# Strassen's two-term sums in the second MLP product of a hybrid decoder layer, with the down weights' sums formed as they are loaded

## The chip, the cores and the metric

The kernel runs on one core of a Trainium2 chip. The metric is the time of one execution on the device in microseconds (us). Three executions of the kernel before took 1248.96 to 1250.3 us, with a median of 1249.71. The engines named below are PE (TensorE, matrix products), DVE (VectorE), ACT (ScalarE), POOL (GpSimd) and SP (SyncE, which issues most DMA transfers).

## The reference

The reference is one layer of a decoder: a normalization, a projection into attention and state-space heads, both mixers, an output projection with a residual, and a squared-ReLU MLP with a second residual. Sequence length and model width are 1024, the hidden width of the MLP is 4096, all in float32. The change lies in the last line.

```python
def _hybrid_layer(x, ...):
    xn = _rmsnorm(x, norm1_g)
    proj = xn @ w_in
    ...
    x = x + mix @ w_out
    hdn = jnp.square(jax.nn.relu(_rmsnorm(x, norm2_g) @ w_mlp_up))
    return x + hdn @ w_mlp_down
```

## The kernel before

The kernel is written as a dataflow over tiles. A planner of the framework, which runs before the program is loaded, turns it into one fixed list of instructions per engine: it takes the instructions in the order of the program as priorities, simulates them with its own costs of operations and transfers, and puts each on its engine's list where the simulation has it ready. An instruction may thus stand far ahead of its place in the program, as early as its tile is free in the simulation. Waits between engines are semaphores that the framework adds. Its costs and due times are not in the trace; the order that came out is.

Every float32 operand of a product is split into a high and a low part (`split`, L77 to L79: ACT copies the high part at L78, DVE subtracts it from the value at L79), and every product of two operands is three matmuls, high by high, high by low, low by high (`mm3`, L106 to L108). All of this is the same before and after.

**Up product** (`up_proj`, run for 16 blocks of 256 hidden features). The product of the up weights with the normalized activations is done in Winograd's form of Strassen's scheme: 2 x 2 blocks, seven products in place of eight. A block loads its up weights as two raw tiles `wm` (L853; the pool `rawp` has two tiles), forms sums of them on DVE (L903, L909, L914, L919), and runs seven products of 12 matmuls each over 512 columns (`psz`, `psx`, `psy`). The activations' sums `X` lie in tiles 0 to 13 of the pools `big_a` and `big_b`. `staggered` interleaves the blocks: the first product of block b+1 stands before the last of block b.

The products give the four quarters of the hidden block, `c11`, `c12`, `c22`, `c21`, each 128 features by 512 tokens. `stage` and `hidden` (L871, L879 to L881) copy, add, and apply the squared ReLU; `keep` (L875) stores a tile to DRAM from POOL's queue. Seven tiles per block are stored, in `d_a[n][i]`: the four quarters or sums of them, as the down product needs them (`comb`, L885, and an addition in place, L923).

In the same function the **down weights** are made ready: a block's rows of `w_down` are loaded as one tile `wd` of 1 MB (L891, issued by SP, in tiles 14 and 15 by turns), four subtractions in place on DVE (L907, L912, L917, L925) turn its quarters into Winograd's sums, and the tile is stored to DRAM as `d_t` (L926, issued by POOL).

**Down product** (`down_proj`). Again seven products, each of 8 steps over pairs of blocks. A step loads two operands of 512 KB each (L973: stored hidden tiles, L974: a quarter of the raw weights or of `d_t`), both into one tile `raw` of 1 MB. Twelve such tiles turn (`RAW`: 14 and 15, then the tiles of `X` as block 15's products let go of them). ACT and DVE split both operands into tiles `ud` (128 x 1024 elements each; the pool `wp` has five tiles), and PE runs 24 matmuls into four PSUM banks. After the last step of a product `gather` (L999) adds each of the four banks to rows of the output tile `x2`, and where the output is done SP stores it (L1001). The residual `x2` is loaded in eight transfers (L1011) after the first step. The first step is placed before block 15's last product.

Of the kernel before, what the change touches and what calls it, by code (L numbers as in the profile page):

```python
# [8 lines left out]
F32 = mybir.dt.float32  # L9
F32R = mybir.dt.float32r  # L10
AF = mybir.ActivationFunctionType
OP = mybir.AluOpType
# [22 lines left out]
def hybrid_layer_kernel(ctx: ExitStack, tc: tile.TileContext, io: dict, out: bass.AP):  # L35
    nc = tc.nc
    PE, ACT, DVE, POOL = nc.tensor, nc.scalar, nc.vector, nc.gpsimd

    consts = ctx.enter_context(tc.tile_pool(name="consts", bufs=1))
    dram = ctx.enter_context(tc.tile_pool(name="dram", bufs=1, space=bass.MemoryType.DRAM))  # L40
    rawp = ctx.enter_context(tc.tile_pool(name="rawp", bufs=2))
    wp = ctx.enter_context(tc.tile_pool(name="wp", bufs=5))
# [4 lines left out]
    for nm, (o, shp) in PACK.items():  # L47
        n = math.prod(shp)
# [18 lines left out]
    d_x2 = [dram.tile([128, 1024], F32, name=f"d_x2{t}") for t in range(8)]  # L67

    d_a = [[dram.tile([2, 128, 512], F32, name=f"d_a{n}_{i}") for i in range(7)] for n in range(8)]
    d_t = [dram.tile([2, 128, 2, 1024], F32, name=f"d_t{n}") for n in range(8)]  # L70

    def rsqrt(out_, in_, mul, n):
        v = consts.tile([128, 8], F32, tag="rsq", name="rsq", bufs=4)
# [3 lines left out]
    def split(h, l, src, eng=DVE):  # L77
        ACT.activation(h, src, AF.Copy)  # L78
        eng.tensor_tensor(l, src, h.bitcast(F32), op=OP.subtract)  # L79
# [45 lines left out]
    def place(n, shape, dtype, name):  # L125
        return (big_a if n < 6 else big_b[0]).tile(shape, dtype, tag=f"g{n}", name=name)
# [720 lines left out]
    HS, H3 = 2, 4  # L847
    def up_proj(blk):

        raw = []  # L850
        for kh in range(2):
            r = rawp.tile([128, 1024], F32, tag="raw", name=f"wm{blk}_{kh}")
            nc.sync.dma_start(out=r, in_=io["w_up"][blk, :, kh])  # L853
# [13 lines left out]

        def stage(tag, ps=None):
            st = half(tag, "st")
            if ps is not None:  # L870
                ACT.activation(st, ps, AF.Copy)  # L871
            return st

        def keep(i, st):
            POOL.dma_start(out=d_a[blk // 2][i][blk % 2], in_=st)  # L875

        def hidden(st, ps):
            if ps is not None:
                DVE.tensor_tensor(st, st, ps, op=OP.add)  # L879
                ACT.activation(st, st, AF.Relu)  # L880
            ACT.activation(st, st, AF.Square)  # L881

        def comb(tag, i, a, b):
            o = half(tag, "comb")
            DVE.tensor_tensor(o, a, b, op=OP.subtract)  # L885
            keep(i, o)
            return o


        wd = place((14, 15)[blk % 2], [128, 2, 1024], F32, f"wd{blk}")  # L890
        nc.sync.dma_start(out=wd, in_=io["w_down"][blk])  # L891
        b11, b12, b21, b22 = wd[:, 0, :512], wd[:, 0, 512:], wd[:, 1, :512], wd[:, 1, 512:]

        z = tr_bank("psz")
        prod(z, a12, B21, True, HS if blk == 0 else 4)
        yield
        x = s_bank("psx")
        prod(x, a11, B11, True, HS if blk == 0 else 4)
        c11 = stage("t", x)
        hidden(c11, z)  # L900
        keep(0, c11)
        yield
        DVE.tensor_tensor(a21, a21, a22, op=OP.add)  # L903
        y = mm_bank("psy")
        prod(y, a21, T1, True, H3 if blk == 0 else 4)
        c22 = stage("x2", y)
        DVE.tensor_tensor(b12, b12, b11, op=OP.subtract)  # L907
        yield
        DVE.tensor_tensor(a21, a21, a11, op=OP.subtract)  # L909
        prod(x, a21, T2, False)  # L910
        c12 = stage("xs", x)
        DVE.tensor_tensor(b22, b22, b12, op=OP.subtract)  # L912
        yield
        DVE.tensor_tensor(a12, a12, a21, op=OP.subtract)  # L914
        prod(y, a12, B22, False)
        hidden(c12, y)
        DVE.tensor_tensor(b11, b22, b11, op=OP.subtract)  # L917
        yield
        DVE.tensor_tensor(a11, a22, a21, op=OP.subtract)  # L919
        prod(x, a11, T3, False)  # L920
        hidden(c22, x)
        keep(2, c22)
        DVE.tensor_tensor(c12, c12, c22, op=OP.add)  # L923
        keep(3, c12)
        DVE.tensor_tensor(b21, b21, b22, op=OP.subtract)  # L925
# [12 lines left out]
    def staggered(gens):  # L938
# [18 lines left out]
    def half_unit():  # L957
# [2 lines left out]
            halves.extend((u[:, 1], u[:, 0]))  # L960
        return halves.pop()

    x2 = []
    RAW = (14, 15, 2, 3, 0, 1, 8, 6, 7, 9, 4, 5)
    X2 = (10, 11, 12, 13)

    def down_proj():


        def prod(ps, i, b, start, after=None):  # L970
            for n in range(8):
                raw = place_turn(RAW, [128, 2, 2, 512], F32, "raw")
                nc.sync.dma_start(out=raw[:, 0], in_=d_a[n][i].rearrange("b p m -> p b m"))  # L973
                nc.sync.dma_start(out=raw[:, 1], in_=b(n))  # L974
                u = []
                for o in range(2):
                    u.append(wp.tile([128, 2, 2, 512], F32R, tag="w", name="ud"))
                    split(u[o][:, 0], u[o][:, 1], raw[:, o])
                ua, ub = u
                for pos in range(4):  # L980
                    pp = slice(pos * 128, pos * 128 + 128)
                    for f in range(2):
                        mm3(ps[pos], ua[:, 0, f, pp], ua[:, 1, f, pp], ub[:, 0, f], ub[:, 1, f],
                            start and n == 0 and f == 0, n == 7 and f == 1, not start)
                    if n == 7:
                        for g in after:
                            gather(ps, pos, *g)
                yield

        def wq(kh, dh):  # L990
            return lambda n: io["w_down"][2 * n:2 * n + 2, :, kh, dh * 512:dh * 512 + 512].rearrange("b p m -> p b m")

        def tq(kh, dh):
            return lambda n: d_t[n][:, :, kh, dh * 512:dh * 512 + 512].rearrange("b p m -> p b m")

        def gather(ps, pos, th, dh, last=False):
            t = 2 * pos + th
            cc = slice(dh * 512, dh * 512 + 512)
            DVE.tensor_tensor(x2[t][:, cc], x2[t][:, cc], ps[pos], op=OP.add)  # L999
# [12 lines left out]
        yield from p2  # L1012
# [77 lines left out]
```

## Time and profile before

| what | value |
|---|---|
| median of three executions | 1249.71 us |
| the profiled execution | 1249.52 us |
| its span, first to last instruction | 1247.7 us |
| mean granted clock of PE | 0.957 |
| busy share of the span: PE, DVE, ACT, POOL | 92%, 66%, 48%, 29% |
| DMA moved in the span | 239.73 MB, 192 GB/s |
| first up-weight split, last matmul of the up product | 586.6 us, 944.2 us |
| first and last matmul of the down product | 936.2 us, 1243.4 us |

The profile is that of one execution. Its page gives busy time per engine, a picture of the span in 40 slices, the DMA queues, the chain of work that ended last, and groups of instructions by line, engine and tile. Other views list single instructions in order of time, total waits of one engine for another, and sums over stretches of time. A busy PE is not PE at its peak: matmuls overlap, so the count of matmuls per microsecond says more than the busy share. A name such as `raw<-d_a` reads: tile `raw` written from `d_a`.

### The profile page before, as it was taken

To read this page: it belongs to the slowest core of one execution; us is meant where nothing else is said; L and a number is where in the kernel's file an instruction comes from. 1 tells how busy PE (TensorE), PEld (TensorE's weight loads), DVE (VectorE), ACT (ScalarE), POOL (GpSimd) and SP (SyncE) were. 2 spreads that over 40 slices of the span, in tenths; PEclk is the share of its full clock that TensorE was granted. 3 is DMA by queue.
4 is the path that set the end of the run, shared out by engine and by line. 5 is a ranking of instruction groups with operands and counts; after the bars stand their busy time and mean duration, and the time that the engine had idled before them with its cause. 6 is when DMAs were issued, how large, how long until landed. Compare 5 with 4: busy or idle time off the path is not lost.

```text
span 1247.7 us, 16686 instructions
## 1 busy us (share of the span) xinstructions
PE 1148.6 (92%) x5734; PEld 961.9 (77%) x5734; DVE 818.2 (66%) x1553; ACT 599.2 (48%) x1276; POOL 363.4 (29%) x544
## 2 busy tenths in 40 slices
PE   6766989999999999999798789999999999999998
PEld 4555777898998887778687567888888888888887
DVE  7998875667666687668887666656554554554453
ACT  5221243777777785434545444555553333333332
POOL 6595732444545464123321112112111000000000
PEclk9887886999999999899999989999999999999999
DMA  7733441635353426654589887444459966555500
GB/s 283 285 101 95 150 132 42 211 140 167 138 203 111 160 97 211 209 185 160 197 312 360 290 323 270 146 150 166 147 213 401 385 216 217 191 184 197 169 34 34
DMA packets 94821, 239.73 MB, mean 192 GB/s; under 512 B 8720, under 2 KB 27664, under 8 KB 85776
## 3 DMA queue, kind: packets, MB, share of 16 engines
q1 hardware_dynamic: 76560, 149.94, 35.7%
q0 software_dynamic: 16736, 85.99, 18.5%
q10 hardware_dynamic: 1440, 2.73, 0.6%
q8 instruction: 45, 0.74, 0.2%
q14 instruction: 40, 0.33, 0.1%
HBM read 164.74 MB, written 73.89 MB: 191 GB/s over the span
## 4 chain that ended last, share of the span: by engine, by line
PE 60%; DVE 12%; DMA 10%; issue 8%; POOL 5%; ACT 4%; SPq 0%; ACTq 0%; POOLq 0%; DVEq 0%
PE psx L107 7%; PE psx L108 7%; PE psx L106 7%; PE psy L106 4%; PE psy L107 4%; PE psy L108 4%; DMA wm<-in_w_up_dram 3%; PE pso L576 3%; PE psq L108 2%; PE psq L106 2%; PE psq L107 2%; PE pss L542 2%; PE psz L106 2%; DMA d_t<-wd 2%; PE psz L107 2%
## 5 line engine op out<-in xcount | busy, mean ns | idle before, releaser
L79 DVE TENSOR_TENSOR ud<-raw,ud 128x1024 fp32r<-128x1024 f32 x112 | 133.0, 1222 | 156.7 <-ACT ud L78 156.7
L78 ACT ACTIVATE ud<-raw 128x1024 fp32r<-128x1024 f32 x112 | 113.0, 1053 | 187.9 <-PE psx L108 103.6
L106 PE MATMUL psx<-X,wu 128*128 128x512 f32 (+1 forms) x260 | 101.9, 392 | 9.3 <-ACT st L871 6.8
L108 PE MATMUL psx<-X,wu 128*128 128x512 f32 (+1 forms) x260 | 101.5, 390 | 0.5 <-DVE wu L79 0.5
L107 PE MATMUL psx<-X,wu 128*128 128x512 f32 (+1 forms) x260 | 101.2, 389 | 0.7 <-DVE X L79 0.7
L78 ACT ACTIVATE wu<-wm 128x512 fp32r<-128x512 f32 x112 | 67.3, 626 | 70.6 <-DMA wm<-in_w_up_dram 37.1
L106 PE MATMUL psx<-ud 128*128 128x512 f32 x256 | 99.6, 389 | 0.0
L107 PE MATMUL psx<-ud 128*128 128x512 f32 x256 | 99.6, 389 | 0.0
L108 PE MATMUL psx<-ud 128*128 128x512 f32 x256 | 99.6, 389 | 0.0
L106 PE MATMUL psq<-wq,xt 128*128 128x384 f32 x256 | 93.4, 365 | 0.7 <-DMA xt<-d_x 0.6
L79 DVE TENSOR_TENSOR wu<-wm,wu 128x512 fp32r<-128x512 f32 x112 | 75.7, 695 | 25.9 <-ACT wu L78 25.9
L875 POOL DMA_DIRECT2D d_a<-st x64 | 34.6, 540 | 198.8 <-ACT st L881 185.6
L107 PE MATMUL psq<-wq,xt 128*128 128x384 f32 x256 | 90.6, 354 | 0.3 <-DVE wq L83 0.3
L108 PE MATMUL psq<-wq,xt 128*128 128x384 f32 x256 | 90.8, 354 | 0.0
L106 PEld LDWEIGHTS psx<-X,wu 128*128 128x128 f32 x260 | 49.3, 189 | 21.9 <-ACT st L871 8.1
L550 POOL TENSOR_SCALAR s<-s,dn 128x128 f32<-128x128 f32 (+3 forms) x64 | 50.2, 788 | 47.8 <-DVE dn L549 45.8
L106 PE MATMUL psy<-X,wu 128*128 128x512 f32 x128 | 52.2, 408 | 10.5 <-ACT st L871 10.5
L79 DVE TENSOR_TENSOR pt<-psp,pt 128x128 fp32r<-128x128 f32 (+2 forms) x96 | 51.1, 552 | 16.0 <-ACT pt L78 15.3
L576 PE MATMUL pso<-pt,V 128*128 128x256 f32 x320 | 54.8, 295 | 3.3 <-ACT pt L78 1.8
L107 PEld LDWEIGHTS psx<-X,wu 128*128 128x128 f32 x260 | 49.3, 190 | 10.9 <-DVE X L79 0.9
L108 PEld LDWEIGHTS psx<-X,wu 128*128 128x128 f32 x260 | 49.3, 190 | 10.7 <-DVE wu L79 0.7
L880 ACT ACTIVATE st<-st 128x512 f32<-128x512 f32 x48 | 30.2, 630 | 53.5 <-DVE st L879 52.7
(306 smaller groups left out, 3116.0 us busy)
## 6 DMA issues: line engine op xcount, KB each, us to landing
xt<-d_x POOLq DMA_DIRECT2D x30, 1024.0 KB, 5.2
raw<-d_a SPq DMA_DIRECT2D x56, 512.0 KB, 4.1
wm<-in_w_up_dram SPq DMA_DIRECT2D x32, 512.0 KB, 4.4
wd<-in_w_down_dram SPq DMA_DIRECT2D x16, 1024.0 KB, 6.5
d_t<-wd POOLq DMA_DIRECT2D x16, 1024.0 KB, 6.8
d_a<-st POOLq DMA_DIRECT2D x64, 256.0 KB, 3.6
raw<-d_t SPq DMA_DIRECT2D x32, 512.0 KB, 5.0
d_a<-comb POOLq DMA_DIRECT2D x48, 256.0 KB, 4.8
```

The source lines that it names most:

```text
L78: ACT.activation(h, src, AF.Copy)
L79: eng.tensor_tensor(l, src, h.bitcast(F32), op=OP.subtract)
L106: PE.matmul(ps, lhsT=ah, rhs=bh, start=start, stop=False, skip_group_check=more)
L107: PE.matmul(ps, lhsT=ah, rhs=bl, start=False, stop=False, skip_group_check=more)
L108: PE.matmul(ps, lhsT=al, rhs=bh, start=False, stop=stop, skip_group_check=more)
L542: PE.matmul(ps[:, :cw], lhsT=Qd[a][:, h, b * 128:(b + 1) * 128], rhs=K2[:, h, c0:c0 + cw], start=a == 0, stop=a == 1)
L550: POOL.tensor_scalar(s[:, :n], s[:, :n], dn, 1.0, op0=OP.mult, op1=OP.mult)
L576: PE.matmul(po[:, :256], lhsT=V2[:, k0 + kb, h, :], rhs=pt[:, a, kb, :], start=k0 + kb == 0 and a == 0, stop=k0 + kb == nb - 1 and a == 1)
L875: POOL.dma_start(out=d_a[blk // 2][i][blk % 2], in_=st)
L880: ACT.activation(st, st, AF.Relu)
```

## The change

The second product goes from Winograd's form to Strassen's own, in which no sum has more than two terms. With H for the hidden quarters (first index token half, second feature half) and B for the weights' quarters the seven products are now

- H11 (B12 - B22)
- H22 (B21 - B11)
- (H21 - H11) (B11 + B12)
- (H11 + H12) B22
- (H21 + H22) B11
- (H11 + H22) (B11 + B22)
- (H12 - H22) (B21 + B22)

In `up_proj` the load of `wd`, its four subtractions and the store to `d_t` are gone, and `d_t` with them. The hidden tiles stored are still seven per block; five of them are now sums (four were before). Two of the sums get tiles of their own (`o1`, `o2`), three are written in place over `c12`, `c11` and `c22`; `c11` and `c22` have been stored themselves before that.

In `down_proj` the tile `raw` is cut into two units of 512 KB (`raw_unit`). A step loads one unit of hidden values, one of weights and, in five of the seven products, a second one of weights, which DVE adds to or subtracts from the first (128 x 1024 elements) before the split. The order of the products is the one of the list. Three products gather to two quarters of the output and four to one, so that there are 40 gathers instead of 28. The first product accumulates in the banks that the third one goes on with; the last two share theirs.

```diff
-    d_t = [dram.tile([2, 128, 2, 1024], F32, name=f"d_t{n}") for n in range(8)]
...
-        def comb(tag, i, a, b):
-            o = half(tag, "comb")
-            DVE.tensor_tensor(o, a, b, op=OP.subtract)
+        def comb(i, o, a, b, op):
+            DVE.tensor_tensor(o, a, b, op=op)
             keep(i, o)
-            return o
-
-        wd = place((14, 15)[blk % 2], [128, 2, 1024], F32, f"wd{blk}")
-        nc.sync.dma_start(out=wd, in_=io["w_down"][blk])
-        b11, b12, b21, b22 = wd[:, 0, :512], wd[:, 0, 512:], wd[:, 1, :512], wd[:, 1, 512:]
...
-        DVE.tensor_tensor(b12, b12, b11, op=OP.subtract)
...
-        DVE.tensor_tensor(b22, b22, b12, op=OP.subtract)
...
         hidden(c12, y)
-        DVE.tensor_tensor(b11, b22, b11, op=OP.subtract)
+        comb(N21M11, half("xs", "o1"), c12, c11, SUB)
         yield
...
         hidden(c22, x)
-        keep(2, c22)
-        DVE.tensor_tensor(c12, c12, c22, op=OP.add)
-        keep(3, c12)
-        DVE.tensor_tensor(b21, b21, b22, op=OP.subtract)
-        POOL.dma_start(out=d_t[blk // 2][blk % 2], in_=wd)
-        s2 = comb("xs", 4, c12, c11)
-        comb("x2", 5, c22, s2)
+        keep(N22, c22)
+        comb(N21P22, c12, c12, c22, ADD)
+        comb(N11P22, half("x2", "o2"), c11, c22, ADD)
         yield
         prod(x, a22, T4, False)
         c21 = stage("t")
         ACT.activation(c21, x, AF.Relu)
         hidden(c21, None)
-        keep(1, c21)
-        comb("t", 6, c21, s2)
+        comb(N11P12, c11, c11, c21, ADD)
+        comb(N12M22, c22, c21, c22, SUB)
         yield
...
+        def raw_unit(src):
+            if not spare:
+                r = place_turn(RAW, [128, 2, 2, 512], F32, "raw")
+                spare.extend((r[:, 1], r[:, 0]))
+            r = spare.pop()
+            nc.sync.dma_start(out=r, in_=src)
+            return r
...
-        def prod(ps, i, b, start, after=None):
+        def prod(ps, i, b0, b1, op, start, to):
             for n in range(8):
-                raw = place_turn(RAW, [128, 2, 2, 512], F32, "raw")
-                nc.sync.dma_start(out=raw[:, 0], in_=d_a[n][i].rearrange("b p m -> p b m"))
-                nc.sync.dma_start(out=raw[:, 1], in_=b(n))
-                u = []
-                for o in range(2):
-                    u.append(wp.tile([128, 2, 2, 512], F32R, tag="w", name="ud"))
-                    split(u[o][:, 0], u[o][:, 1], raw[:, o])
-                ua, ub = u
+                ra = raw_unit(d_a[n][i].rearrange("b p m -> p b m"))
+                rb = raw_unit(wd(n, *b0))
+                if b1 is not None:
+                    DVE.tensor_tensor(rb, rb, raw_unit(wd(n, *b1)), op=op)
+                ua, ub = [wp.tile([128, 2, 2, 512], F32R, tag="w", name="ud") for _ in range(2)]
+                split(ua[:, 0], ua[:, 1], ra)
+                split(ub[:, 0], ub[:, 1], rb)
...
-        z = l_banks("psz")
-        p2 = prod(z, 1, wq(1, 0), True, [(0, 0)])
-        next(p2)
+        b11, b12, b21, b22 = (0, 0), (0, 1), (1, 0), (1, 1)
+        x = l_banks("psx")
+        m3 = prod(x, N11, b12, b22, SUB, True, [(0, 1, ADD)])
+        next(m3)
         yield
...
-        x = r_banks("psx")
-        yield from prod(x, 0, wq(0, 0), True, [(0, 0, True)])
-        y = l_banks("psy")
-        yield from prod(y, 3, tq(0, 1), True, [(1, 1)])
-        yield from prod(x, 4, tq(1, 1), False, [(0, 1)])
-        yield from prod(y, 6, wq(1, 1), False, [(0, 1, True)])
-        yield from prod(x, 5, tq(0, 0), False, [(1, 1, True)])
-        yield from prod(x, 2, tq(1, 0), False, [(1, 0, True)])
+        y = r_banks("psy")
+        yield from prod(y, N22, b21, b11, SUB, True, [(0, 0, ADD), (1, 0, ADD)])
+        yield from prod(x, N21M11, b12, b11, ADD, False, [(1, 1, ADD)])
+        y = r_banks("psy")
+        yield from prod(y, N11P12, b22, None, None, True, [(0, 0, SUB), (0, 1, ADD, True)])
+        x = l_banks("psx")
+        yield from prod(x, N21P22, b11, None, None, True, [(1, 0, ADD, True), (1, 1, SUB)])
+        y = r_banks("psy")
+        yield from prod(y, N11P22, b11, b22, ADD, True, [(1, 1, ADD, True)])
+        yield from prod(y, N12M22, b21, b22, ADD, False, [(0, 0, ADD, True)])
```

More of the change, by code (lines that the diff above doesn't have):

```diff
@@ L847, in hybrid_layer_kernel @@
     HS, H3 = 2, 4
+    N11, N22, N21P22, N11P22, N11P12, N21M11, N12M22 = range(7)
     def up_proj(blk):
@@ L881, in hidden @@
             ACT.activation(st, st, AF.Square)
-        def comb(tag, i, a, b):
-            o = half(tag, "comb")
-            DVE.tensor_tensor(o, a, b, op=OP.subtract)
+        def comb(i, o, a, b, op):
+            DVE.tensor_tensor(o, a, b, op=op)
             keep(i, o)
-            return o
-        wd = place((14, 15)[blk % 2], [128, 2, 1024], F32, f"wd{blk}")
-        nc.sync.dma_start(out=wd, in_=io["w_down"][blk])
-        b11, b12, b21, b22 = wd[:, 0, :512], wd[:, 0, 512:], wd[:, 1, :512], wd[:, 1, 512:]
+        ADD, SUB = OP.add, OP.subtract
         z = tr_bank("psz")
@@ L900, in up_proj @@
         hidden(c11, z)
-        keep(0, c11)
+        keep(N11, c11)
         yield
-        DVE.tensor_tensor(a21, a21, a22, op=OP.add)
+        DVE.tensor_tensor(a21, a21, a22, op=ADD)
         y = mm_bank("psy")
@@ L906, in up_proj @@
         c22 = stage("x2", y)
-        DVE.tensor_tensor(b12, b12, b11, op=OP.subtract)
         yield
-        DVE.tensor_tensor(a21, a21, a11, op=OP.subtract)
+        DVE.tensor_tensor(a21, a21, a11, op=SUB)
         prod(x, a21, T2, False)
         c12 = stage("xs", x)
-        DVE.tensor_tensor(b22, b22, b12, op=OP.subtract)
         yield
-        DVE.tensor_tensor(a12, a12, a21, op=OP.subtract)
+        DVE.tensor_tensor(a12, a12, a21, op=SUB)
         prod(y, a12, B22, False)
         hidden(c12, y)
-        DVE.tensor_tensor(b11, b22, b11, op=OP.subtract)
+        comb(N21M11, half("xs", "o1"), c12, c11, SUB)
         yield
-        DVE.tensor_tensor(a11, a22, a21, op=OP.subtract)
+        DVE.tensor_tensor(a11, a22, a21, op=SUB)
         prod(x, a11, T3, False)
         hidden(c22, x)
-        keep(2, c22)
-        DVE.tensor_tensor(c12, c12, c22, op=OP.add)
-        keep(3, c12)
-        DVE.tensor_tensor(b21, b21, b22, op=OP.subtract)
-        POOL.dma_start(out=d_t[blk // 2][blk % 2], in_=wd)
-        s2 = comb("xs", 4, c12, c11)
-        comb("x2", 5, c22, s2)
+        keep(N22, c22)
+        comb(N21P22, c12, c12, c22, ADD)
+        comb(N11P22, half("x2", "o2"), c11, c22, ADD)
         yield
@@ L967, in down_proj, with wd @@
     def down_proj():
-        def prod(ps, i, b, start, after=None):
-            for n in range(8):
-                raw = place_turn(RAW, [128, 2, 2, 512], F32, "raw")
-                nc.sync.dma_start(out=raw[:, 0], in_=d_a[n][i].rearrange("b p m -> p b m"))
-                nc.sync.dma_start(out=raw[:, 1], in_=b(n))
-                u = []
-                for o in range(2):
-                    u.append(wp.tile([128, 2, 2, 512], F32R, tag="w", name="ud"))
-                    split(u[o][:, 0], u[o][:, 1], raw[:, o])
-                ua, ub = u
+        ADD, SUB = OP.add, OP.subtract
+        spare = []
+        def raw_unit(src):
[5 more added lines that the diff above has]
+            return r
+        def wd(n, kh, dh):
+            return io["w_down"][2 * n:2 * n + 2, :, kh, dh * 512:dh * 512 + 512].rearrange("b p m -> p b m")
+        def prod(ps, i, b0, b1, op, start, to):
+            for n in range(8):
+                ra = raw_unit(d_a[n][i].rearrange("b p m -> p b m"))
[5 more added lines that the diff above has]
+                split(ub[:, 0], ub[:, 1], rb)
                 for pos in range(4):
@@ L985, in prod, with gather @@
                     if n == 7:
-                        for g in after:
+                        for g in to:
                             gather(ps, pos, *g)
                 yield
[L990 to L996, printed above, removed]
+        def gather(ps, pos, th, dh, op, last=False):
             t = 2 * pos + th
             cc = slice(dh * 512, dh * 512 + 512)
-            DVE.tensor_tensor(x2[t][:, cc], x2[t][:, cc], ps[pos], op=OP.add)
+            DVE.tensor_tensor(x2[t][:, cc], x2[t][:, cc], ps[pos], op=op)
             if last:
                 nc.sync.dma_start(out=out[t * 128:(t + 1) * 128, cc], in_=x2[t][:, cc])
-        z = l_banks("psz")
-        p2 = prod(z, 1, wq(1, 0), True, [(0, 0)])
-        next(p2)
+        b11, b12, b21, b22 = (0, 0), (0, 1), (1, 0), (1, 1)
+        x = l_banks("psx")
+        m3 = prod(x, N11, b12, b22, SUB, True, [(0, 1, ADD)])
+        next(m3)
         yield
@@ L1011, in down_proj @@
                 nc.sync.dma_start(out=x2[-1], in_=d_x2[2 * n + t])
-        yield from p2
-        x = r_banks("psx")
-        yield from prod(x, 0, wq(0, 0), True, [(0, 0, True)])
-        y = l_banks("psy")
-        yield from prod(y, 3, tq(0, 1), True, [(1, 1)])
-        yield from prod(x, 4, tq(1, 1), False, [(0, 1)])
-        yield from prod(y, 6, wq(1, 1), False, [(0, 1, True)])
-        yield from prod(x, 5, tq(0, 0), False, [(1, 1, True)])
-        yield from prod(x, 2, tq(1, 0), False, [(1, 0, True)])
+        yield from m3
+        y = r_banks("psy")
[8 more added lines that the diff above has]
+        yield from prod(y, N12M22, b21, b22, ADD, False, [(0, 0, ADD, True)])
     staggered([up_proj(b) for b in range(16)])
```

## The prediction

> **What bounds the kernel now.** I read the page's slices first, to see where TensorE (PE) is not full; then windows, to count what it did there; then the waits and the SP queue of that stretch.
>
> ```profile
> PE   6766989999999999999798789999999999999998
> PEclk9887886999999999899999989999999999999999
> DMA  7733441635353426654589887444459966555500
> ```
>
> A slice is 31.2 us. The up projection begins near slice 19. PE is ragged in slices 19 to 23, just where DMA stands at 9, 8, 8, 7, and full from 25 to the end but for the last. Two windows of equal length put a number on it (length, then busy us and count for PE, PEld, DVE, ACT, POOL, then granted clock, DMA share, GB/s):
>
> ```profile
> 600.00:780.00 180.00, 155.47 (x637) 122.91 (x636) 131.47 (x208) 83.98 (x145) 39.19 (x68) 0.94 0.81 295
> 780.00:960.00 180.00, 180.00 (x795) 149.09 (x795) 103.09 (x152) 95.06 (x155) 33.41 (x62) 1.00 0.54 197
> 960.00:1220.00 260.00, 260.00 (x1148) 215.35 (x1147) 128.17 (x120) 96.56 (x96) 0.00 (x0) 1.00 0.57 202
> ```
>
> At a full clock PE starts a matmul of 512 columns every 180/795 = 0.2264 us. In 600 to 780 it ran 158 fewer than in the next 180 us, and 18 of them are the half-wide ones of block 0. The stretch therefore loses 158 x 0.2264 + 18 x 0.113 = 37.8 us against a full PE. From 780 on nothing is lost: up blocks and the whole down product run at PE's own pace, so no saving of DVE or DMA work there can shorten anything. What the stretch 600 to 780 has and the later blocks have not is the down weights' work:
>
> ```profile
> DVE wd L907 <- DMA wd<-in_w_down_dram: 17.0, 7, 3.5
> DVE wm L903 <- DMA wm<-in_w_up_dram: 13.3, 5, 3.7
> ```
>
> ```profile
> SPq L891 <- DMA d_t<-wd: 97.6, 13, 13.6
> SPq L853 <- DVE wu L79: 52.0, 12, 16.0
> ```
>
> ```profile
> 678.37 0.33 SPq L891 DMA_DIRECT2D wd<-in_w_down_dram  x1
> 682.61 0.33 SPq L853 DMA_DIRECT2D wm<-in_w_up_dram  x1
> 688.57 0.33 SPq L891 DMA_DIRECT2D wd<-in_w_down_dram  x1
> 688.99 0.38 SPq L853 DMA_DIRECT2D wm<-in_w_up_dram  x1
> 698.89 12.04 SPq L891 DMA_DIRECT2D wd<-in_w_down_dram  x2
> 711.98 0.33 SPq L853 DMA_DIRECT2D wm<-in_w_up_dram  x1
> ```
>
> (Total us, times, longest.) The load of a block's down weights (L891) waits for its tile until an earlier block's sums are stored (d_t), 97.6 us in all, and SP issues in order: the second of the two up-weight loads that a block needs (L853) leaves at 688.99 and 711.98, each a fraction of a us after a wd load that was waiting. VectorE (DVE) stands 17.0 us in front of a wd tile that has not landed, with splits of up weights behind it. All sixteen wd loads leave between 556.9 and 745.3 us, about two per up block, far ahead of their use:
>
> ```profile
> L891 SPq DMA_DIRECT2D wd<-in_w_down_dram x16: 327/328/383, 556.9 to 745.3; - x16
> ```
>
> **The change, part by part.** First the up stage.
>
> ```profile
> wd<-in_w_down_dram SPq DMA_DIRECT2D x16, 1024.0 KB, 6.5
> d_t<-wd POOLq DMA_DIRECT2D x16, 1024.0 KB, 6.8
> raw<-d_a SPq DMA_DIRECT2D x56, 512.0 KB, 4.1
> d_a<-st POOLq DMA_DIRECT2D x64, 256.0 KB, 3.6
> raw<-in_w_down_dram SPq DMA_DIRECT2D x24, 512.0 KB, 10.0
> x<-d_x SPq DMA_DIRECT2D x8, 512.0 KB, 11.9
> ```
>
> ```profile
> L907 DVE TENSOR_TENSOR wd<-wd 128x512 f32<-128x512 f32 x15 | 11.1, 741 | 17.0 <-DMA wd<-in_w_down_dram 17.0
> L925 DVE TENSOR_TENSOR wd<-wd 128x512 f32<-128x512 f32 x15 | 10.3, 686 | 0.0
> L885 DVE TENSOR_TENSOR comb<-st,comb 128x512 f32<-128x512 f32 x14 | 9.6, 687 | 2.2 <-ACT st L881 2.2
> ```
>
> Gone are 16 loads and 16 stores of 1 MB, 33.6 MB, nearly all out of the stretch that moves 295 GB/s x 180 us = 53 MB, and 64 subtractions of the weights; 15 blocks' worth stand in the stretch, four lines at 11.1 and about 10.3 us, 42 us of the 131.5 that DVE is busy there. Added is one sum of hidden values per block (five where there were four): 16 x 0.687 = 11 us of DVE over the stage, beside PE, since DVE is idle 77 of 180 us in the full stretch. The seven stores per block stay seven. So each block will look like those of 780 to 960, which lose nothing: the term is **-37.8 us**. What I leave standing is block 0's own start (PE waits there for operands still being split, and the first reload of up weights has only two tiles to turn in); I take **+4 us** for it, between 0 and the 37.8 that stay if the weights' work was not the cause, near the low end because the full blocks have the same reload and hide it.
>
> One wait is new. The last sum, N12M22, is written over c22, whose store must have landed first:
>
> ```profile
> 862.58 0.54 POOL L875 DMA_DIRECT2D d_a<-st  x1 [9.28 <-ACT st L881]
> ```
>
> ```profile
> 866.34 0.64 ACT L881 ACTIVATE st<-st 128x512 f32<-128x512 f32 x1
> ```
>
> In this block the store of c22 leaves at 862.58 and lands by the median 3.6 us later, 866.2; c21, the sum's other operand, is ready at 866.98. The store is 0.8 us early. Were it 2 us late, the next block's splits would stand behind it on DVE, which is idle 43% of the time: 0 taken, 2 x 16 = 32 us as the far end if no slack took it up. The other sums in place write over c11, stored five products before, and c12, not stored.
>
> The down stage issues the same 7 x 8 steps of 24 matmuls, 24 x 0.2264 = 5.43 us of PE each (the third window above gives 260/1148 = 0.2265 a matmul). New are a third load of 512 KB and a DVE sum of 128x1024 in 5 of 7 products, 40 steps, and 40 gathers instead of 28.
>
> ```profile
> L79 DVE TENSOR_TENSOR ud<-raw,ud 128x1024 fp32r<-128x1024 f32 x112 | 133.0, 1222 | 156.7 <-ACT ud L78 156.7
> ```
>
> ```profile
> 1021.84 1.23 DVE L79 TENSOR_TENSOR ud<-raw,ud 128x1024 fp32r<-128x1024 f32 x1 [3.08 <-ACT ud L78]
> 1022.99 1.28 DVE L999 TENSOR_TENSOR x<-x,psx 128x512 f32<-128x512 f32 x2
> 1024.18 1.22 DVE L79 TENSOR_TENSOR ud<-raw,ud 128x1024 fp32r<-128x1024 f32 x1
> 1025.32 0.68 DVE L999 TENSOR_TENSOR x<-x,psx 128x512 f32<-128x512 f32 x1
> 1026.19 0.69 DVE L999 TENSOR_TENSOR x<-x,psx 128x512 f32<-128x512 f32 x1 [0.19 <-PE psx L108]
> ```
>
> The sum has the size, engine and two SBUF inputs of the split's row, so 1.22 us: a step then asks DVE for 3 x 1.22 = 3.7 of 5.43 us, hidden. At the end of a product with two gathers per position DVE gets 8 x 0.64 = 5.1 us more in about two steps (10.9 us against 12.4): 1.5 us of lag. The splits lead PE by more than a step (in the rows above a split follows ScalarE's copy at once, then DVE idles 3.08 us a step), so I take 0.5 us for the three such ends together. Loads: 1.57 MB per 5.43 us is 289 GB/s.
>
> ```profile
> 960.00:1000.00 40.00, 40.00 (x178) 33.12 (x177) 19.01 (x18) 15.10 (x16) 0.00 (x0) 1.00 1.05 385
> ```
>
> The same kinds of load ran at 385 GB/s when queued, so the steady flow fits. The raw tiles now hold 24 units, 8 steps ahead instead of 12. The tight place is the start: 12.6 MB for the first product and 4.2 MB of x2 take 16.8/385 = 44 us, PE needs 8 x 5.43 = 43, and the loads start only some six products of block 15 (6 x 12 x 0.2264 = 16 us) earlier, beside its seven stores. I take 2 us for it; 0 if the lead holds, 14 if it fails (the 11.9 us that an x2 load took to land, and a slow clock after the stop). Together **+2.5 us**. The last gather and the last store are as before.
>
> ```profile
> 615.68 0.49 PE L106 MATMUL psx<-X,wu 128*128 128x512 f32 x1 [0.78 <-DVE st L879]
> 619.89 0.80 PE L106 MATMUL psz<-X,wu 128*128 128x512 f32 x1 [3.72 <-ACT wu L78]
> ...
> 624.32 0.59 PE L107 MATMUL psz<-X,wu 128*128 128x512 f32 x1
> 624.75 0.41 PE L108 MATMUL psz<-X,wu 128*128 128x512 f32 x1
> ```
>
> The slow clock is seen here: after 3.72 us idle PE takes 4.86 us (619.89 to 624.75) for eleven matmuls that take 2.49 at a full clock, so a stop of that length costs 2.4 us more. [...]
>
> **Sum** against the profiled execution (1249.5 us, span 1247.7; the median of the three runs is 1249.7, the same): 1249.5 - 37.8 + 4 + 2.5 = **1218 us**.
>
> **Rivals.** *Late sums at the start of the down product.* A weight sum waits for a landing, as the wd subtraction did; queued ahead of the splits of the current step it stops them. For: the 17.0 us of L907, and landings of 10.0 us in the fill against 4.1 later. Against: it is over once the lead is built. It adds 6 us (one sum late by 10.0 - 4.1 = 5.9) to 23 (three of them, two with a slow clock of 2.4 behind): 1224 to 1241, with 1230 as the value.
>
> *The reload of the up weights is the bound.* The 52.0 us of L853 behind DVE do not name wd; if half the loss is this, 19 us of the 37.8 stay instead of 4, and the time is 1233. Against: the full stretch reloads the same two tiles.
>
> *Slower: the sum closes a loop through the raw tiles.* If the planner puts the sum of the step eight ahead before the next step's splits, and its loads leave only when the splits just done free a tile, the loop is load 4.1 + sum 1.22 + two splits 2.44 = 7.8 us instead of 5.43: 2.3 us per step. The tile turns (three units a step, two to a tile) make this likely in at most every second step of the 40: 20 x 2.3 = 46, 1264 us. It decides from (1249.5 - 1218)/2.3 = 14 steps on. For: wd did just this on SP and DVE. Against: when both are ready the split is the older work, and the landing falls after it by 1 to 2 us. [...]
>
> *The traffic only moves.* 33.6 MB leave the up stage, 21 MB come to the down stage; if stops there gave back what the up stage gains, 1249.
>
> **Chances.** Forecast 1218 (1211 to 1224): 0.58. Late sums, 1230 (1224 to 1241): 0.17. Reload, 1233: 0.11. Slower, 1264: 0.09. No change: 0.05. The range runs from 1211 (neither the 4 nor most of the 2.5 us) to 1241, the far end of the late sums, which takes in the reload and leaves the last two out. A measurement here tells about 0.2% (2.5 us) from no change: faster 0.86, same 0.05, slower 0.09.
>
> **What would show it.** Right: in the changed profile PE is full from block 1 on, no wait of SP for a d_t store, DVE waits for wm only; the down stage starts some 34 us earlier and runs at 0.2264 us per matmul with DVE 3.7 us a step. Wrong: PE idle in the first two down products behind "ACT ud", with DVE waiting for DMA raw (late sums, or the loop if it goes on in every two-term product); or the up stage still ragged behind DMA wm (reload).

## The result, and the profile after

| | kernel before | changed kernel |
|---|---|---|
| executions | 4 | 4 |
| median, lowest and highest (us) | 1250.01, 1248.96 to 1251.6 | 1214.85, 1214.02 to 1220.95 |
| the profiled execution, its span (us) | 1249.52, 1247.7 | 1220.95, 1219.2 |

The ratio is 0.9728, with a 95% interval of 0.9695 to 0.9762: 35 us less, where 31.7 were forecast, and 3 us under the forecast time. The profiled execution of the changed kernel is the longest of its four; the others took 1214.0 to 1215.0.

The page's slices of the changed kernel (30.5 us each), and its windows (length, busy us and count for PE, PEld, DVE, ACT, POOL, then granted clock, DMA share, GB/s):

```profile
PE   6766989999999999999999999999999999999998
...
DMA  7734432635355425753244434434379999575930
```

```profile
600.00:660.00 60.00, 55.54 (x249) 44.02 (x248) 44.25 (x67) 34.45 (x61) 12.98 (x19) 1.00 0.40 136
660.00:780.00 120.00, 120.00 (x531) 99.38 (x530) 75.93 (x120) 65.80 (x114) 24.39 (x45) 1.00 0.45 163
780.00:880.00 100.00, 100.00 (x443) 82.81 (x442) 65.39 (x104) 56.11 (x97) 20.23 (x38) 1.00 0.42 150
880.00:1000.00 120.00, 118.83 (x523) 97.71 (x523) 79.44 (x82) 48.71 (x58) 7.40 (x14) 1.00 0.96 356
1000.00:1200.00 200.00, 200.00 (x884) 165.62 (x883) 126.23 (x120) 73.49 (x74) 0.00 (x0) 1.00 0.66 231
```

The ragged slices are gone, and the lower clock with them: the granted clock was 0.94 in 600 to 780 before and is 1.00 now. At most (1 - 0.94) x 180 = 10.8 us of the loss there, an estimate, came from the lower clock, the rest from PE's stops. From 660 to 880 PE runs 974 matmuls in 220 us, one per 0.226 us, as it did before only from 780 on. DMA is lightly used there (163 and 150 GB/s) and the heavy traffic (356 GB/s) stands in 880 to 1000, where the down product's tiles fill.

Whole executions differ by some us in their first half, whose program the change leaves as it is, so I compare stages by marks of the trace. The first product of a block is `psz`. The row of its high-by-high matmuls gives the start of the first of them in block 0 and of the last of them in block 15. The last `ud` matmul is the last of PE's work. The view of one tile, the changed kernel and then the kernel before (count, shortest/median/longest ns, first and last start):

```profile
L105 PE MATMUL psz<-X,wu x68: 280/389/389, 597.7 to 888.9; 128*128 128x512 f32 x60, 128*128 128x256 f32 x8
...
L107 PE MATMUL psy<-ud x256: 388/389/389, 954.4 to 1214.8; 128*128 128x512 f32 x128
```

```profile
L106 PE MATMUL psz<-X,wu x68: 274/389/796, 596.9 to 919.2; 128*128 128x512 f32 x60, 128*128 128x256 f32 x8
...
L108 PE MATMUL psx<-ud x256: 388/389/389, 982.9 to 1243.4; 128*128 128x512 f32 x128
```

The **up stage**, from the first mark to the second, went from 919.2 - 596.9 = 322.3 us to 888.9 - 597.7 = 291.2, so 31.1 less. In both traces PE starts 1233 matmuls of 512 columns and 31 of 256 between these marks. At 0.2264 us each, and at 0.113 for the half-wide ones (half of it, an estimate; in the changed kernel's trace they follow 0.12 us apart from 600.08 to 601.15), they take 282.7 us, so 39.6 us were lost there before and 8.5 are lost now. The **tail**, from there to the last matmul, went from 324.2 to 325.9, so 1.7 more. Together that is 29.4 us less; the changed kernel reached its up stage 0.8 later, which leaves the 28.6 between the two profiled executions. That the medians lie 35 apart, 6 more, is not seen in these two traces.

Of the waits in the up stage (SP's queue, 600 to 880) those for `d_t` are gone, and SP now waits for the up weights' own tiles:

```profile
SPq L853 <- DVE wu L78: 245.8, 30, 16.4
SPq L969 <- DMA d_a<-st: 6.5, 2, 6.4
SPq L853 <- DMA wm<-in_w_up_dram: 5.6, 3, 3.0
```

The 1.7 us of the tail have their place in DVE's list of instructions (start, duration, idle time before and what ended it), a few us into the down product:

```profile
909.06 1.22 DVE L980 TENSOR_TENSOR raw<-raw 128x1024 f32<-128x1024 f32 x1 [2.67 <-DMA raw<-in_w_down_dram]
910.20 1.22 DVE L78 TENSOR_TENSOR ud<-raw,ud 128x1024 fp32r<-128x1024 f32 x1
911.34 0.68 DVE L884 TENSOR_TENSOR o<-st 128x512 f32<-128x512 f32 x1
911.94 0.68 DVE L879 TENSOR_TENSOR st<-st,psx 128x512 f32<-128x512 f32 x1
```

```profile
DVE raw L980 <- DMA raw<-in_w_down_dram: 28.7, 19, 3.4
...
PE psx L105 <- DVE st L879: 1.2, 1, 1.2
DVE st L884 <- DMA d_a<-st: 0.5, 1, 0.5
```

A weight sum (L980) waits 2.67 us for its landing. Block 15's own addition, L879, which lets go of a bank that PE needs, stands behind it, and PE loses 1.2 us. From 880 on DVE waits 28.7 us in 19 places for landings of down weights, but only this one reaches PE. The last row is the new wait of the sum written over `c22`: 0.5 us, once.

### The profile page after: what moved, and what is told of

Read it like the earlier page. It is cut to its first block, busy times and chain, and to the rows that moved or that the text cites. A ratio compares the mean times of both kernels' runs of the same rounds, so it can differ in the third digit from the quotient of the medians.

```text
span 1219.2 us, 16630 instructions
## 1 busy us (share of the span) xinstructions
PE 1139.4 (93%) x5734; PEld 956.7 (78%) x5734; DVE 841.0 (69%) x1557; ACT 598.6 (49%) x1276; POOL 354.8 (29%) x528
## 4 chain that ended last, share of the span: by engine, by line
PE 70%; DVE 11%; DMA 6%; issue 5%; POOL 4%; ACT 4%; SPq 0%; ACTq 0%; DVEq 0%; POOLq 0%
PE psx L105 7%; PE psx L106 7%; PE psx L107 7%; PE psy L105 7%; PE psy L106 7%; PE psy L107 7%; PE pso L575 3%; PE psq L107 2%; PE psq L105 2%; PE psq L106 2%; PE pss L541 2%; PE psp L564 2%; PE psy L438 1%; PE pso L107 1%; PE pso L105 1%
## 5 line engine op out<-in xcount | busy, mean ns | idle before, releaser
L105 PE MATMUL psy<-ud 128*128 128x512 f32 x256 | 99.6, 389 | 0.0
L106 PE MATMUL psy<-ud 128*128 128x512 f32 x256 | 99.6, 389 | 0.0
L107 PE MATMUL psy<-ud 128*128 128x512 f32 x256 | 99.6, 389 | 0.0
L875 POOL DMA_DIRECT2D d_a<-st x80 | 43.5, 544 | 130.1 <-DVE st L884 65.9
L106 PE MATMUL psx<-ud 128*128 128x512 f32 x192 | 74.8, 390 | 0.0
L105 PE MATMUL psx<-ud 128*128 128x512 f32 x192 | 74.7, 389 | 0.0
L107 PE MATMUL psx<-ud 128*128 128x512 f32 x192 | 74.7, 389 | 0.0
L980 DVE TENSOR_TENSOR raw<-raw 128x1024 f32<-128x1024 f32 x40 | 49.7, 1249 | 28.7 <-DMA raw<-in_w_down_dram 28.7
L105 PEld LDWEIGHTS psx<-X,wu 128*128 128x128 f32 x260 | 48.8, 188 | 16.5 <-ACT st L871 4.6
```

Of the source, the lines that this page charges most:

```text
L105: PE.matmul(ps, lhsT=ah, rhs=bh, start=start, stop=False, skip_group_check=more)
L106: PE.matmul(ps, lhsT=ah, rhs=bl, start=False, stop=False, skip_group_check=more)
L107: PE.matmul(ps, lhsT=al, rhs=bh, start=False, stop=stop, skip_group_check=more)
L980: DVE.tensor_tensor(rb, rb, raw_unit(wd(n, *b1)), op=op)
```

## The experiments

The profile says that the up stage gained, not which part of the weights' work had cost it. The theory on record: SP's queue order and DVE's waiting for `wd`. The rivals for the up stage: the bytes alone, or DVE's work alone. For the down stage: late sums, the loop through the raw tiles, or nothing. Ratios are to the kernel before on the same chip, with their 95% intervals. "Up" is the stage between the two `psz` marks of the profiled execution, "tail" what follows.

| kernel | median us | ratio | up us | tail us |
|---|---|---|---|---|
| before | 1250.0 | 1 | 322.3 | 324.2 |
| changed | 1214.9 | 0.9728 [0.9695, 0.9762] | 291.2 | 325.9 |
| u1: all of the weights' work back | 1256.0 | 1.0056 [1.0032, 1.0079] | 328.8 | 325.6 |
| u2: load and store back, no sums | 1242.1 | 0.9947 [0.9926, 0.9967] | 312.6 | 325.8 |
| u3: sums back, nearly no transfers | 1222.4 | 0.9796 [0.9771, 0.9821] | 292.3 | 326.1 |
| u4: as u2, loads issued by POOL | 1243.2 | 0.9954 [0.9933, 0.9975] | 310.7 | 326.3 |
| u6: as u2, each load tied to its block | 1223.7 | 0.9803 [0.9765, 0.9840] | 294.5 | 327.0 |
| u7: before, each load tied to its block | 1250.0 | 1.0009 [0.9986, 1.0032] | 325.5 | 324.1 |
| b1: before without the weights' work | 1213.0 | 0.9699 [0.9666, 0.9731] | 287.9 | 324.1 |
| v1: more tiles for up weights | 1216.1 | 0.9746 [0.9706, 0.9786] | 287.4 | 325.9 |
| d1: third load kept, no sum | 1216.0 | 0.9743 [0.9711, 0.9774] | 289.7 | 324.1 |
| d2: no third load, no sum | 1211.9 | 0.9709 [0.9672, 0.9745] | 289.8 | 324.1 |
| d3: every weight sum twice | 1217.6 | 0.9754 [0.9719, 0.9788] | 290.2 | 326.4 |
| d4: six raw tiles in place of twelve | 1216.4 | 0.9748 [0.9718, 0.9777] | 290.3 | 325.9 |

The kernels that share the changed kernel's up blocks (d1 to d4) have up stages of 289.7 to 290.3 us, so a difference of 2 us and more in this column is a difference of the kernel; their first `psz`, however, starts anywhere from 590.9 to 596.8 us, which is why a median tells less. A stage length, on the other side, is that of one execution; that of u1 is the longest of its nine, 7 us above their median.

### The whole, and its two halves

**u1, all back.** The changed kernel with the weights' work put into `up_proj` again; nothing reads the stored sums.

```diff
+        wd = place((14, 15)[blk % 2], [128, 2, 1024], F32, f"wd{blk}")
+        nc.sync.dma_start(out=wd, in_=io["w_down"][blk])
...
+        DVE.tensor_tensor(b12, b12, b11, op=SUB)
...
+        DVE.tensor_tensor(b22, b22, b12, op=SUB)
...
+        DVE.tensor_tensor(b11, b22, b11, op=SUB)
...
+        DVE.tensor_tensor(b21, b21, b22, op=SUB)
+        POOL.dma_start(out=d_t[blk // 2][blk % 2], in_=wd)
```

> The changed kernel with the whole work on the down weights put back into the up stage (load of wd, four sums, store to d_t); the down product does not read d_t, it goes on with the new form. Theory of the prediction (that work alone made PE ragged between 600 and 780 us): 1245 to 1252 us, 30 to 37 above the changed kernel's 1214.9. Rival (the gain comes from elsewhere, as the new list order or the freed tiles): under 1235.

**u2, traffic only.** As u1 without the four subtractions.

> The changed kernel with the load of wd and the store to d_t put back, without the four sums; what is stored is not read. Theory Q (SP's queue: up-weight loads behind wd loads that wait for a store): most of the loss returns, 1235 to 1250 us. Theory V (DVE: sums that wait for a landing stand ahead of the splits): 1215 to 1222 us.

**u3, sums only.** As u1 without the load and the store of each block: two tiles are loaded once, and the blocks' sums run on them.

```diff
+    for i in range(2):
+        wds.append(place((14, 15)[i], [128, 2, 1024], F32, f"wd{i}"))
+        nc.sync.dma_start(out=wds[i], in_=io["w_down"][i])
...
+        wd = wds[blk % 2]
```

> The changed kernel with the four sums per block put back on DVE, over two tiles that are loaded once; no load and no store per block, and the sums' values are not used. Theory Q: within 4 us of the changed kernel, 1213 to 1219 us, since nothing waits for a transfer. Theory V in its plain form (42 us of DVE work in the stretch are too much beside the splits): 1225 us or more.

**b1, before without the weights' work.** `up_proj` of the kernel before without `wd`, and its down product reading raw quarters, so that Winograd's sums of the weights are left out.

```diff
-        wd = place((14, 15)[blk % 2], [128, 2, 1024], F32, f"wd{blk}")
-        nc.sync.dma_start(out=wd, in_=io["w_down"][blk])
...
-            return lambda n: d_t[n][:, :, kh, dh * 512:dh * 512 + 512].rearrange("b p m -> p b m")
+            return wq(kh, dh)
```

> The kernel before without the work on the down weights; its down product reads raw quarters of w_down where it read d_t, so Winograd's sums of the weights are left out. It has the old down form (two loads a step, 28 gathers, no sums) behind an up stage without the weights' work. If the new down form is hidden, as forecast (at most 2.5 us): 1211 to 1216 us. If the sums in the down product cost more (late sums): under 1208 us.

Measured: 1255.96, 1242.12, 1222.42 and 1212.97 us. u1 lies 4 us above the range set for it, b1 within its own, and u2 where the theory of SP's queue had put it. The rows of `psz`, u1, u2, u3 and b1, one kernel each:

```profile
L107 PE MATMUL psz<-X,wu x68: 277/389/796, 602.5 to 931.3; 128*128 128x512 f32 x60, 128*128 128x256 f32 x8
```

```profile
L107 PE MATMUL psz<-X,wu x68: 281/389/628, 596.4 to 909.0; 128*128 128x512 f32 x60, 128*128 128x256 f32 x8
```

```profile
L105 PE MATMUL psz<-X,wu x68: 278/389/497, 597.9 to 890.2; 128*128 128x512 f32 x60, 128*128 128x256 f32 x8
```

```profile
L105 PE MATMUL psz<-X,wu x68: 278/389/390, 597.6 to 885.5; 128*128 128x512 f32 x60, 128*128 128x256 f32 x8
```

The weights' work is the cause: put back it costs 37.6 us of up stage (328.8 - 291.2), and the kernel before without it has an up stage of 287.9. It is not DVE's work by itself: the 64 subtractions on tiles that lie there add 1.1 us to the up stage (7.6 to the median, between the two bounds that had been set, so that by the median it fits neither; the other 6.5 us are not in the up stage, and the profiled execution of u3 is only 1.4 us above that of the changed kernel). The transfers alone add 21.4. The two parts added, 22.5, do not make the whole, 37.6: beside the transfers the sums cost 16.2 (u1 against u2), where resident ones cost 1.1. The sign is safer than the size: by the medians the parts give 27.3 + 7.6 = 34.9 and the whole 41.1. Some of it is PE's clock: granted 0.95 in 600 to 880 of u1 and 0.98 there in u2, against 1.00 in u3 and the changed kernel. The difference of 0.03 on 280 us makes 8 us, an estimate of the most that it cost.

### Is it SP's order?

**u4.** As u2, but POOL issues the loads of `wd`, so that no load of up weights stands behind one that waits.

```diff
-        nc.sync.dma_start(out=wd, in_=io["w_down"][blk])
+        POOL.dma_start(out=wd, in_=io["w_down"][blk])
```

> As the run with load and store of wd and without sums (1242.1 us), but the load of wd is issued by POOL instead of SP. Theory Q (it is SP's order: up-weight loads stand behind wd loads that wait for a store): 1214 to 1222 us, since the bytes stay and the queue is free. Rival (it is the DMA engines' load): 1235 to 1245, as with SP.

Measured: 1243.15 us, as u2. SP's queue in the up stage of u4, then its engines' waits there:

```profile
SPq L855 <- DVE wu L80: 225.2, 28, 16.4
SPq L855 <- DMA wm<-in_w_up_dram: 21.3, 6, 7.0
SPq L975 <- DMA d_t<-wd: 14.0, 2, 12.9
```

```profile
ACT wu L79 <- DMA wm<-in_w_up_dram: 47.3, 16, 6.6
DVE wm L902 <- DMA wm<-in_w_up_dram: 41.3, 14, 7.3
```

SP has no wait of a `wd` load any more (u2 has 58.1 us of them), and the up weights are still late: ACT and DVE wait 88.6 us for them (47.3 + 41.3; 27.0 + 25.7 in the changed kernel). The order in SP's queue, which the prediction named first, is not what cost the 20 us of the transfers. Whether it costs something where the sums are there too was not tried.

### Is it the bytes, or when they come?

The windows of u2 show something that the sum of bytes hides:

```profile
640.00:660.00 20.00, 17.85 (x71) 14.36 (x72) 13.57 (x23) 10.69 (x20) 4.31 (x8) 0.91 0.98 372
660.00:680.00 20.00, 17.03 (x74) 13.44 (x72) 8.14 (x13) 6.31 (x11) 3.76 (x7) 1.00 0.99 370
...
740.00:760.00 20.00, 20.00 (x90) 16.57 (x89) 12.34 (x21) 9.48 (x17) 4.62 (x9) 1.00 0.41 149
```

```profile
L922 POOL DMA_DIRECT2D d_t<-wd x16: 537/538/651, 563.8 to 709.3; - x16
L891 SPq DMA_DIRECT2D wd<-in_w_down_dram x16: 327/328/425, 556.7 to 702.9; - x16
```

The last of the sixteen stores leaves at 709.3, in the first half of the stage. Nothing ties a load to its block but a free tile, so the planner runs ahead. From 600 to 680 the DMA engines stand at a share of 0.90 to 0.99 and PE runs 70 to 74 matmuls per 20 us; from 740 on, at 0.41, it runs 90. How late the up weights come shows in their own loads. For those of 600 to 700 us the time from issue to landing is, in u2 and then in u6, a run that the next paragraphs explain:

```profile
DMA to landing us min/median/max: 4.7/7.8/11.4
```

```profile
DMA to landing us min/median/max: 3.4/4.6/7.1
```

The median is 8.3 us in u4 and 3.8 in the changed kernel. A high share alone does not stop PE in the same 20 us (u1 has 90 matmuls in 640 to 660 at a share of 0.96); what counts, as far as these rows tell, is how late the loads come that its operands hang on.

**u6.** As u2, with four columns of the block's up weights copied into the tile ahead of the load: the load cannot start before its block's up weights are there.

```diff
+        DVE.tensor_copy(wd[:, 0, :4], a11[:, :4])
         nc.sync.dma_start(out=wd, in_=io["w_down"][blk])
```

> The changed kernel with the down weights' load and store put back into the up blocks as in the first traffic kernel (no sums, the copy is read by nobody), and a copy of four columns of the block's up weights into the tile ahead of the load, so that each load can start only when its own block's up weights have landed: the same 33.6 MB, but one block's worth per block instead of sixteen blocks' worth in the first half of the stage. Theory bunching (the loss is that of a stretch in which the DMA engines stand at a share of 0.9 to 0.99 and the up weights land late): 1214 to 1226 us, PE at 88 to 90 matmuls per 20 us through 640 to 880, DMA share 0.6 to 0.85 all along. Theory bytes (each byte beside the up stage costs, wherever it lies): 1236 to 1248 us, as the first traffic kernel's 1242.

**u7.** The same line in the kernel before, sums included.

> The kernel before with that one copy of four columns ahead of the load of the down weights, and nothing else changed: all of the weights' work stays, loads, sums and stores, but its load is tied to its own block. Theory bunching: 1214 to 1232 us (the sums alone cost 8 us, the traffic then little), so that most of the change's gain could be had without it. Theory bytes, or theory that bytes and sums cost by their amount: 1244 to 1256 us, no better than the 1249 of before.

Measured: u6 1223.68, u7 1250.04 us. Two windows of u6 and its `psz`:

```profile
640.00:660.00 20.00, 19.26 (x84) 15.31 (x83) 12.72 (x21) 11.83 (x21) 4.77 (x9) 1.00 0.77 281
660.00:680.00 20.00, 19.95 (x87) 15.91 (x86) 14.71 (x25) 11.62 (x20) 3.88 (x8) 1.00 0.74 258
```

```profile
L107 PE MATMUL psz<-X,wu x68: 274/389/389, 594.4 to 888.9; 128*128 128x512 f32 x60, 128*128 128x256 f32 x8
```

Without sums the theory of bunching holds in the main: the same 33.6 MB, at shares of 0.6 to 0.85 all along, cost 3.3 us of up stage instead of 21.4. PE runs 84 to 90 matmuls per 20 us from 640 on, where 88 to 90 were expected, and the tail is 1.1 longer; the median is 8.8 us above the changed kernel's. With sums it does not carry over. In u7 the loads are spread and nothing is gained; its time is the one that the rival had forecast:

```profile
L106 PE MATMUL psz<-X,wu x68: 281/389/792, 592.5 to 918.0; 128*128 128x512 f32 x60, 128*128 128x256 f32 x8
```

```profile
DVE wd L891 <- DMA wm<-in_w_up_dram: 50.7, 14, 5.6
ACT wu L78 <- DMA wm<-in_w_up_dram: 47.4, 19, 4.9
...
DVE wd L908 <- DMA wd<-in_w_down_dram: 12.2, 11, 2.0
```

Its up stage is 325.5 us, 3.2 more than before, and the loss lies in every block (PE has 82 to 86 matmuls per 20 us from 740 to 880, where the kernel before is full from 780). DVE waits for landings in both places, 50.7 us at the tying copy (16.0 in u6) and 12.2 at the first sum. With both, the splits of up weights stand behind, and they free the two tiles that the next load needs. The up weights land late in u7 too, 5.8 us after issue in the median of all 32 loads, against 4.4 in u6 and in the kernel before. How much of u7's loss is the copy's own wait was not separated, so u7 does not show that spreading is useless with sums, only that this way of spreading is.

### Up weights: what is left of the stage

**v1.** The changed kernel with the up weights of every second block in tiles 14 and 15.

```diff
+        wm2 = place((14, 15)[blk // 2 % 2], [128, 2, 1024], F32, f"wm{blk}") if blk % 2 else None
         for kh in range(2):
-            r = rawp.tile([128, 1024], F32, tag="raw", name=f"wm{blk}_{kh}")
+            r = rawp.tile([128, 1024], F32, tag="raw", name=f"wm{blk}_{kh}") if wm2 is None else wm2[:, kh]
```

> The changed kernel, with the up weights of every second block in tiles 14 and 15, which stand free in the up stage, so that up weights can land one block earlier. If the 5 us that the changed kernel loses between 600 and 660 us are late up weights (block 0's start stays, as forecast): 1208 to 1213 us and 262 to 266 matmuls in 600 to 660. If they are the matrix products' own order at the seam of the stages, or the copies of x: 1214 to 1217 us and about 249.

Measured: 1216.08 us in 6 executions (1212.88 to 1224.09). Its `psz`:

```profile
L105 PE MATMUL psz<-X,wu x68: 278/389/389, 596.1 to 883.5; 128*128 128x512 f32 x60, 128*128 128x256 f32 x8
```

The up stage is 287.4 us, 3.8 less than in the changed kernel and 2.3 to 2.9 less than in d1 to d4, which have its up blocks. PE has 262 matmuls in 600 to 660 in place of 249, but v1's stage began 1.6 us earlier; in 620 to 660 it has 178, a full PE, against 159 (160 to 163 in d1 to d4). So the loss there was the wait for up weights in two tiles. The median does not show it: the time is the one forecast for the other case, the changed kernel's within the interval. It is not a better version that these runs can tell.

### The down stage

**d1, no sum; d2, no third load and no sum; d3, every sum twice; d4, six raw tiles.**

```diff
-                    DVE.tensor_tensor(rb, rb, raw_unit(wd(n, *b1)), op=op)
+                    raw_unit(wd(n, *b1))
```

> The changed kernel with the third load of a step kept and its sum on DVE left out (the products use one raw quarter). Prediction (sums hidden, 2.5 us for the whole down stage): 0 to 3 us faster than the changed kernel, 1211 to 1216. Rival (late sums cost): 5 us faster or more, 1210 or less.

```diff
-                if b1 is not None:
-                    DVE.tensor_tensor(rb, rb, raw_unit(wd(n, *b1)), op=op)
```

> The changed kernel without the third load and without the sum in the down stage's first products: 16.8 MB and 40 sums less; the sum of weights is left out, so that the output isn't the reference's. Forecast's theory (they lie beside a full PE): 1212 to 1217 us, within 3 us of the changed kernel's 1214.9. Late-sums rival (the load and the sum cost where the down stage starts): 1205 to 1211 us.

```diff
+                    rc = raw_unit(wd(n, *b1))
+                    DVE.tensor_tensor(rb, rb, rc, op=op)
-                    DVE.tensor_tensor(rb, rb, raw_unit(wd(n, *b1)), op=op)
+                    DVE.tensor_tensor(rb, rb, rc, op=op)
```

> The changed kernel with each weight sum done twice on DVE (the second quarter is added or subtracted twice, so the values differ): DVE is asked for 4.9 us of the 5.43 of a step. Prediction (PE keeps its pace as long as DVE's work fits in a step and the raw tiles lead): 0 to 6 us more, 1215 to 1221. Loop theory (landing, sums and two splits follow one another in every second step, 4.1 + 2.44 + 2.44 = 9 us): 1235 or more.

```diff
-    RAW = (14, 15, 2, 3, 0, 1, 8, 6, 7, 9, 4, 5)
+    RAW = (14, 15, 2, 3, 0, 1)
```

> The changed kernel with 6 raw tiles in the down product instead of 12: loads lead by 4 steps instead of 8. If the lead of eight steps is needed to hide landings of 8 to 9 us: 15 us more or worse, 1230 and up. If two or three steps of 5.43 us are enough: within 5 us, 1213 to 1220.

d1 and d2 leave the second quarter out of the weights' sums, d3 takes it in twice. Measured: 1216.03, 1211.91, 1217.61 and 1216.44 us. The tails separate them better: 324.1, 324.1, 326.4 and 325.9 us, against 325.9 of the changed kernel and 324.2 of before. The group of the doubled sums in d3:

```profile
L981 DVE TENSOR_TENSOR raw<-raw 128x1024 f32<-128x1024 f32 x40 | 49.8, 1248 | 18.7 <-DMA raw<-in_w_down_dram 18.6
L982 DVE TENSOR_TENSOR raw<-raw 128x1024 f32<-128x1024 f32 x40 | 48.9, 1222 | 0.7
```

The sum costs 1.8 us, all at the start; the third load costs nothing (d1 has it, d2 has not, both 324.1). Forty sums more, 48.9 us of DVE, add 0.5, and half the raw tiles add nothing: no loop through the tiles is seen at either size. d2's median lies 3 us under the changed kernel, just outside what either theory gave it; 1.8 of them are the tail. The rest is not in what d2 changes: its profiled execution reaches its first `psz` 6.8 us earlier than that of the changed kernel.

## Why the prediction held

**The loss of 37.8 us is the down weights' work, and goes with it.** Right. In the traces 31.1 us went between the marks, where -37.8 and +4 make 33.8, and u1 and b1 tie this to the work itself (37.6 back, 287.9 without). One reading on the way is off: slices 19 to 23, where PE is ragged, have DMA at 5, 8, 9, 8, 8. The sum rests on the windows and is not touched by it.

**How that work costs.** This part of the reading was wrong where it was put most firmly. SP's queue did hold loads of up weights behind waiting loads of `wd`, but u4 took that away and 19.5 of the 21.4 us stayed. The 97.6 us of SP's wait marked the time that the tile's store took; without the sums it was no price. What the runs put in its place: the planner had packed all sixteen blocks' transfers into half the stage, and with the DMA engines at a share of 0.90 to 0.99 (u2, 600 to 680) the up weights landed late (7.8 us after issue in u2, 4.6 in u6, for losses of 21.4 and 3.3). The row of the sixteen `wd` loads, 556.9 to 745.3, was quoted as "far ahead of their use" and not followed further. The second reading, DVE standing before a `wd` that has not landed, with splits behind it, fits the 16.2 us that sums cost on top of the transfers and the 1.1 that they cost without; it was not isolated, and the size is uncertain, as said above. The forecast did not depend on which of these it was, because it took the whole work away.

**+4 for block 0's start and two tiles.** 6.7 measured in the prediction's own window: 17 matmuls fewer than a full PE, and 25 of them half-wide, make 17 x 0.2264 + 25 x 0.113.

```profile
600.00:780.00 180.00, 175.54 (x778) 143.40 (x777) 120.19 (x186) 100.25 (x174) 37.37 (x64) 1.00 0.43 154
```

v1 shows 2.3 to 3.8 of it to be the up weights' two tiles. One piece was unforeseen: the planner put the first weight sum of the down product into block 0, some 300 us ahead of its use.

```profile
608.14 2.31 DVE L980 TENSOR_TENSOR raw<-raw 128x1024 f32<-128x1024 f32 x1
```

**0 for the new wait over `c22`.** 0.5 us, once, and PE did not wait.

**+2.5 for the down stage.** 1.7 measured. The gathers, for which 0.5 was taken, cost nothing to be seen (d1 has 40 of them and the tail of b1, which has 28). The start, for which 2 was taken, cost 1.7 to 1.8, by the mechanism of the late-sums rival: a sum waits for a landing with block 15's addition behind it. Its price was put at 6 to 23; the wait was 2.67 us, not 5.9, and PE did not stop at the other eighteen waits. The down product started 30.3 us earlier (905.9 against 936.2), where some 34 were expected.

**The sum.** From the profiled execution before, the terms give -31.3; the traces give -29.4, the medians -35. So by the traces the sum of the terms is right to 2 us, and the further 6 us of the medians, which no term foresaw, have no place in a trace. They could lie ahead of the up stage, which kernels with the same program there reached at times 7 us apart. That the median comes out 3 us under the forecast, and the profiled execution 3 us over it, is chance as far as these runs show.

**The rivals.** Reload of the up weights: real, but 2.3 to 3.8 us, not 15. Loop through the raw tiles: refuted by d3 and d4. Traffic only moves: it did move, 0.96 of the DMA engines in 880 to 1000, and PE lost 1.2 us there. The clock in 600 to 660 was 0.93 before and is 1.00 after, where the longest stop of PE is 1.62 us. In the kernel before, the stop of 3.72 us quoted in the prediction was followed by a slow clock (0.52 in 619.89 to 625), and so was one of 2.58 us (0.64 in 757.2 to 762; the rows stand at the end).

## What to carry to other kernels

Where a stage is ragged, look first at when its transfers leave compared with when they are used: here a planner that ran ahead into free tiles had filled the DMA engines (to a share of 0.99 in u2) and made the urgent loads late (7.8 us to landing, 4.6 in u6), and the long wait of SP's queue (58.1 us in u2) was only the mark of it. Price a piece of work by taking it out whole before taking sides on how it costs: transfers and the sums on them cost less apart than together (22.5 and 37.6 us by the traces, 34.9 and 41.1 by the medians). The operations that wait for a landing cost little here behind a stock of ready work (sums twice over: 0.5 us) and showed at the seam where there was none yet (1.2 us of PE).

## What the runs showed of the hardware

- From issue to landing, a load of 512 KB took 9.0 us in the down product of the changed kernel (the median of the down weights' loads), against 3.7 us in the up stage. In 880 to 1000, at a DMA share of 0.96, the loads into `raw` took 10.8 us, in 1000 to 1200, at 0.66, 5.3:

```profile
raw<-in_w_down_dram SPq DMA_DIRECT2D x96, 512.0 KB, 9.0
...
wm<-in_w_up_dram SPq DMA_DIRECT2D x32, 512.0 KB, 3.7
```

- The core moved 398 GB/s in its busiest slice.

```profile
GB/s 288 272 115 106 151 112 70 211 114 178 129 155 170 143 96 166 243 191 121 75 159 173 167 145 165 145 140 167 144 294 398 387 387 352 193 240 183 333 140 35
```

- The first weight sum took 2.31 us at 608.14 where the forty of them average 1.249; what slowed this one is not shown.

- In the kernel before, PE's clock fell after a stop of 2.58 us (granted 1.00 in 740 to 757.2, 0.64 in 757.2 to 762). The matmuls that follow it start 0.43 us apart, where 0.226 is the full pace. A stop of 3.28 us that ended at 701.4 was not followed by a lower clock (1.00 in 700 to 720), so the length of a stop alone does not decide it.

```profile
757.16 0.50 PE L106 MATMUL psy<-X,wu 128*128 128x512 f32 x1 [2.58 <-ACT st L871]
...
758.45 0.63 PE L107 MATMUL psy<-X,wu 128*128 128x512 f32 x1
758.88 0.63 PE L108 MATMUL psy<-X,wu 128*128 128x512 f32 x1
```
